# A row maximum over 64 MB: three blocks of rows per partition in place of two

## The chip, the core and the metric

The kernel runs on one core of a Trainium2 chip. The metric is the device time of one execution in microseconds (us), as the median of several runs. Lower is better.

## What is computed

The input `x` has the shape 32 x 512 x 1024 in float32 (67.11 MB). The output is the maximum over the last axis, 32 x 512 in float32.

```python
def reference(x):
    return np.max(x, axis=-1).astype(np.float32)
```

There are 16384 rows of 1024 values (4 KB each). Each value is read once, and one value per row is written.

## The kernel before, in words

**Layout.** The 16384 rows are dealt out to 128 partitions, so that each partition holds 128 rows. This is not done in one piece: the list `BLOCKS` (line 13) cuts the 128 rows of a partition into blocks. A block of S rows per partition covers 128 x S consecutive rows of `x`, and partition p gets rows p x S to p x S + S - 1 of it. So S decides the distance in `x` between the data of neighbouring partitions, the partition pitch: S x 4 KB. Before the change there are two blocks, of 112 rows (pitch 448 KB) and of 16 rows (14 in the list and 2 cut into pieces; pitch 64 KB).

**Loads.** Each number in a block's list is one load: so many rows of every partition, 128 runs of 4 KB times that number. Eighteen loads (line 238) and four pieces (line 243) are issued by SyncE's queue, in order. `loads[j]` is numbered from 0 through all blocks. The pieces are the last two rows, each cut in two by `PIECES` (line 26).

**The ring.** The loads go into `ring`, which has room for `RING = 47` rows per partition. Loads take places one behind another, and start again at 0 when the next one does not fit. `issue()` (line 231) sends the next load as soon as, in the written order of the program, all readers of the rows that it overwrites have been written down; on the chip SyncE then waits for those readers (VectorE's reductions) and for the earlier load into that place. A load that waits holds up all loads behind it in SyncE's queue.

**Work.** `PLAN` (line 31) is the written order of the steps: `d` reduces the rows of a load on VectorE (`direct`, a `reduce_max` on line 78), `t` moves some of the rows by TensorE, ScalarE and GpSimd instead (`turn`: transposes on line 160, a copy on line 166, an all-reduce over partitions on line 168), `b` brings these results back (line 178), `p` has VectorE reduce the remaining columns of a shared row, `m` merges, and `f0` to `f3` reduce the four pieces. `SHARED` and `RANK` say for loads 10, 13, 14 and 17 how many rows and how many of their eight column parts go the second way. The numbers in `PLAN`, `SHARED` and `RANK` are those of the loads in order, whatever block they are in.

**Stores.** Results of all rows stand in `res`, one column per row of a partition. `views` holds one store for each block. All but the last are issued on ScalarE's queue (line 265) and made to wait for the first piece's reduction (`behind`); the last (line 267) waits for the final merge.

The lines that cannot be said in words:

```python
BLOCKS = [
    [2, 15, 16, 14, 11, 11, 10, 10, 8, 8, 7],
    [3, 3, 3, 2, 1, 1, 1],
]
RING = 47
```

```python
for sizes in BLOCKS:
    S = sum(sizes) + last * (sizes is BLOCKS[-1])
    xb = xf[first * P:(first + S) * P, :].rearrange("(p i) d -> p i d", p=P)
    dst = bass.AP(tensor=of.tensor, offset=of.offset + first * P, ap=[[S, P], [1, S]])
    views.append((dst, res[:, first:first + S]))
```

Of the kernel before, what the change touches and what calls it, by code (L numbers as in the profile page):

```python
# [10 lines left out]


BLOCKS = [
    [2, 15, 16, 14, 11, 11, 10, 10, 8, 8, 7],
    [3, 3, 3, 2, 1, 1, 1],
]
RING = 47
# [279 lines left out]
```

## Time and profile before

| what | value |
|---|---|
| median of 3 runs | 163.83 us (163.79 to 163.84) |
| span of the profiled execution, first to last instruction | 162.1 us |
| DMA queue of the loads (q1) | 67.11 MB, 96.8% of the 16 engines' span |
| HBM read over the span | 67.11 MB; 414 GB/s with the stores |
| VectorE (DVE) busy | 135.3 us, 83% |
| GpSimd (POOL), TensorE (PE), ScalarE (ACT) busy | 15.9, 13.6 and 6.3 us |
| mean granted TensorE clock | 0.955 |

The profile is taken of one execution. Its span counts from the first instruction of the program to the last; the device time of an unprofiled run, 163.83 us, is 1.7 us longer, and what lies around the span is not in the trace. Engines are named PE (TensorE matmul), PEld (TensorE weight load), DVE (VectorE), ACT (ScalarE), POOL (GpSimd) and SP (SyncE); a q behind the name is the engine's instruction queue, where DMAs are issued. "L78" is line 78 of the kernel. A group's row has the line, the engine, the operation, output and input with their shapes, the count, then busy time and mean duration. A row of the timeline or the chain begins with its start and its duration in us. A row of DMA issues has the count, the KB of one, and the time in us from issue to landing. A row of windows has the stretch, its length, the busy time of PE, PEld, DVE, ACT and POOL, then the granted clock, the busy share of the DMA engines (above 1 where packets overlap or where their time reaches past the window) and GB/s.

### The profile page before, as it was taken

What the parts mean: (1) busy time and instruction counts of PE and PEld (TensorE: products, weight loads), DVE (VectorE), ACT (ScalarE), POOL (GpSimd) and SP (SyncE); (2) the same over time, 40 slices, a digit from 0 to 9 for tenths busy, and PEclk for the clock granted to TensorE, in tenths of its full rate; (3) what the DMA queues carried; (4) which work ended last, traced back from release to release, by engine and by line L of the source; (5) the groups of instructions that cost most, each with busy time, mean ns of one, the idle gap of its engine ahead of it and who ended that gap; (6) DMA issues with size and microseconds to landing.
All of it is one profiled execution on the core that took longest, in us unless ns stands there. A gap on an engine that the chain in (4) does not pass through costs nothing.

```text
span 162.1 us, 295 instructions
## 1 busy us (share of the span) xinstructions
PE 13.6 (8%) x76; PEld 11.7 (7%) x76; DVE 135.3 (83%) x33; ACT 6.3 (4%) x7; POOL 15.9 (10%) x10
## 2 busy tenths in 40 slices
PE   0000000000000000000000000000000000772942
PEld 0000000000000000000000000000000000762731
DVE  3500019998399999999999999996999999999994
ACT  3000000000000000000000000000000000241120
POOL 0000000000000000000000000000000000099791
PEclk9999999999999999999999999999999999996555
DMA  5995999599879999898999799799999989999991
GB/s 178 566 485 258 470 501 517 259 517 517 354 340 439 453 404 534 356 523 367 478 411 475 334 485 475 334 485 388 477 429 388 466 382 446 415 421 416 411 388 34
DMA packets 3456, 67.18 MB, mean 414 GB/s; under 512 B 640, under 2 KB 896, under 8 KB 1536
## 3 DMA queue, kind: packets, MB, share of 16 engines
q1 hardware_dynamic: 3168, 67.11, 96.8%
q10 hardware_dynamic: 288, 0.07, 0.2%
HBM read 67.11 MB, written 0.07 MB: 414 GB/s over the span
## 4 chain that ended last, share of the span: by engine, by line
DMA 50%; DVE 47%; SPq 1%; issue 0%; DVEq 0%
DMA ring<-in_x_dram 50%; DVE ring L78 45%; DVE joint L78 2%; SPq L238 1%; DVEq L292 0%
## 5 line engine op out<-in xcount | busy, mean ns | idle before, releaser
L78 DVE TENSOR_REDUCE ring<-ring 128x1 f32<-128x1024 f32 (+13 forms) x20 | 129.9, 6547 | 23.5 <-DMA ring<-in_x_dram 23.5
L168 POOL PARTITION_ALL_REDUCE top<-sb x6 | 15.7, 2658 | 142.6 <-ACT sb L166 142.5
L160 PE MATMUL ps<-ident,ring 128*128 128x128 f32 x38 | 9.0, 423 | 140.0 <-DMA ring<-in_x_dram 140.0
L160 PEld LDWEIGHTS ps<-ident,ring 128*128 128x128 f32 x38 | 7.6, 225 | 140.1 <-issue 140.1
L166 ACT COPY sb<-ps 128x1024 f32<-128x1024 f32 (+2 forms) x6 | 5.0, 834 | 150.5 <-PE ps L160 143.5
L78 DVE TENSOR_REDUCE joint<-ring 128x2 f32<-128x1280 f32 (+1 forms) x3 | 3.9, 1314 | 0.0
L178 PE MATMUL got<-ident,top 1*128 1x1 f32 x24 | 2.7, 228 | 3.8 <-POOL top L168 3.6
L178 PEld LDWEIGHTS got<-ident,top 1*128 1x128 f32 x24 | 2.4, 188 | 4.6 <-POOL top L168 4.6
L178 PE MATMUL joint<-ident,top 1*128 1x1 f32 x14 | 2.0, 244 | 1.9 <-POOL top L168 1.9
L178 PEld LDWEIGHTS joint<-ident,top 1*128 1x128 f32 x14 | 1.7, 210 | 2.7 <-POOL top L168 2.7
L166 ACT ACT_TABLE_LOAD x1 | 1.3, 1283 | 0.7 <-PEq L281 0.7
L83 DVE MEMSET ident<- 128x128 f32 x1 | 0.2, 165 | 0.8 <-PEq L281 0.8
L90 DVE TENSOR_SCALAR rowno<-rowno 32x1 f32<-32x1 f32 x3 | 0.4, 146 | 0.1
L85 DVE TENSOR_TENSOR_SCAN colno<-ident 128x128 f32<-128x128 f32 x1 | 0.4, 425 | 0.0
L92 DVE TENSOR_SCALAR ident<-colno,rowno 128x128 f32<-128x128 f32 x1 | 0.3, 288 | 0.0
L87 DVE STREAM_TRANSPOSE rowno<-colno 128x32 f32<-128x32 f32 x1 | 0.2, 211 | 0.0
L78 DVE TENSOR_REDUCE ring<-got 128x3 f32<-128x24 f32 x1 | 0.2, 172 | 0.0
L78 DVE TENSOR_REDUCE ring<-joint 128x5 f32<-128x20 f32 x1 | 0.2, 170 | 0.0
L281 POOL MEMSET const-float32-0.0<- 128x1 f32 x1 | 0.1, 98 | 0.2 <-issue 0.2
L281 POOL MEMSET const-bfloat16-1.0<- 128x1 bf16 x1 | 0.1, 102 | 0.0
L281 POOL MEMSET const-uint8-127<- 128x1 uint8 x1 | 0.1, 101 | 0.0
L281 POOL MEMSET const-float32-1.0<- 128x1 f32 x1 | 0.1, 98 | 0.0
(1 smaller groups left out, 0.1 us busy)
## 6 DMA issues: line engine op xcount, KB each, us to landing
ring<-in_x_dram SPq DMA_DIRECT2D x2, 5632.0 KB, 29.9
ring<-in_x_dram SPq DMA_DIRECT2D x2, 5120.0 KB, 36.8
ring<-in_x_dram SPq DMA_DIRECT2D x2, 4096.0 KB, 32.5
ring<-in_x_dram SPq DMA_DIRECT2D x1, 7680.0 KB, 22.6
ring<-in_x_dram SPq DMA_DIRECT2D x1, 7168.0 KB, 58.0
ring<-in_x_dram SPq DMA_DIRECT2D x3, 1536.0 KB, 35.7
ring<-in_x_dram SPq DMA_DIRECT2D x1, 3584.0 KB, 29.2
ring<-in_x_dram SPq DMA_DIRECT2D x2, 1024.0 KB, 17.8
```

The lines of the kernel that those rows point to most:

```text
L78: return in_turn("DVE", nc.vector.reduce_max(out=out, in_=in_, axis=X))
L83: in_turn("DVE", nc.vector.memset(ident, 1.0))
L85: in_turn("DVE", nc.vector.tensor_tensor_scan(out=colno, data0=ident, data1=ident, initial=-1.0, op0=ALU.add, op1=ALU.mult))
L87: in_turn("DVE", nc.vector.transpose(out=rowno, in_=colno[:, :32]))
L90: in_turn("DVE", nc.vector.tensor_scalar(out=part, in0=part, scalar1=float(q * 32), scalar2=None, op0=ALU.add))
L92: identity = in_turn("DVE", nc.vector.tensor_scalar(out=ident, in0=colno, scalar1=rowno[:, 0:1], scalar2=None, op0=ALU.is_equal))
L160: in_turn("PE", nc.tensor.transpose(out=ps[:, w:w + P], in_=rows(j)[:, lead[j] + r + i, c * P:(c + 1) * P], identity=ident,))
L166: in_turn("ACT", nc.scalar.copy(out=sb[:, :W], in_=ps[:, :W]))
L168: in_turn("POOL", nc.gpsimd.partition_all_reduce(top[:, :W], sb[:, :W], P, bass_isa.ReduceOp.max))
L178: in_turn("PE", nc.tensor.transpose(out=share(j)[:, r + i, c:c + 1], in_=tops[k][0:1, w:w + P], identity=ident[0:1, 0:1],))
L238: load = nc.sync.dma_start(out=rows(issued), in_=src)
L281: nc = _bacc.Bacc("TRN2", target_bir_lowering=False, num_devices=1)
```

## The change

The 112 rows of the first block are divided into a block of 16 rows and one of 96. The loads of the first block are now of 2 and 14 rows, and the second block begins with 16, 14 and 12 rows where 16, 14 and 11 stood. The numbers of the loads, `PLAN`, `SHARED`, `RANK`, the ring's size, the last block and the pieces stay as they are. Since each block has its own store, there are three stores in place of two. Every line below the list moves down by one (line 78 becomes 79, and so on).

```diff
 BLOCKS = [
-    [2, 15, 16, 14, 11, 11, 10, 10, 8, 8, 7],
+    [2, 14],
+    [16, 14, 12, 11, 10, 10, 8, 8, 7],
     [3, 3, 3, 2, 1, 1, 1],
 ]
 RING = 47
```

The partition pitch in `x` is 64 KB for loads 0 and 1, 384 KB for loads 2 to 10, and 64 KB for loads 11 to 17 and the pieces. The places in the ring move with the sizes: loads 0 to 3 take rows 0 to 46 of 47, load 4 (12 rows) begins again at 0, load 5 at 12, load 6 at 23, load 7 at 33, and load 8 at 0 again.

## The prediction

> **What bounds the kernel now.** I read the page first, for the share of the DMA queue and of the engines.
>
> ```profile
> span 162.1 us, 295 instructions
> PE 13.6 (8%) x76; PEld 11.7 (7%) x76; DVE 135.3 (83%) x33; ACT 6.3 (4%) x7; POOL 15.9 (10%) x10
> ...
> q1 hardware_dynamic: 3168, 67.11, 96.8%
> q10 hardware_dynamic: 288, 0.07, 0.2%
> ```
>
> The load queue (q1) keeps the sixteen DMA engines busy for 96.8% of the span; VectorE (DVE), the next, for 83%. So the stream of loads should be the bound, and VectorE only follows. The chain that ended last names VectorE for nearly half of its length, so I checked it in order of time.
>
> ```profile
> 1.62 41.49 DMA ring<-in_x_dram
> ...
> 43.13 66.55 DVE ring L78 x5
> ...
> 111.01 38.94 DMA ring<-in_x_dram
> ...
> 159.14 0.59 DVE ring L78
> 159.74 0.09 DVEq L292
> ```
>
> The 66.55 us on VectorE are a stretch in which both run; at its end VectorE's release lets SyncE issue four loads, and the last of them takes 38.94 us to land, behind others, so this link is not a lack of work in the queue. To see whether the queue ever runs dry I set the issue of each gated load (timeline of SyncE's queue) beside the landing of the load ahead of it (issue plus the time to landing, from the DMA view of the same stretch). Two answers of the DMA view, for the issues at 60.76 and at 75.37:
>
> ```profile
> ring<-in_x_dram SPq DMA_DIRECT2D x1, 5120.0 KB, 38.1
> ring<-in_x_dram SPq DMA_DIRECT2D x1, 5120.0 KB, 35.6
> ```
>
> They land at 98.9 and 111.0: 12.1 us apart for 10 rows, although they were issued 14.6 us apart. In the same way the load issued at 60.38 lands 26.3 us later, and its predecessor lands only at 39.96 + 33.4 = 73.4, 13 us after that issue. This is the smallest lead of all gated loads. The queue is never empty from the first packet to the last piece.
>
> What a row costs follows from the starts of the first reductions, each released by its load:
>
> ```profile
> 5.65 2.29 DVE L78 TENSOR_REDUCE ring<-ring 128x2 f32<-128x2048 f32 x1 [3.14 <-DMA ring<-in_x_dram]
> 23.78 16.15 DVE L78 TENSOR_REDUCE ring<-ring 128x15 f32<-128x15360 f32 x1 [15.85 <-DMA ring<-in_x_dram]
> 43.13 17.22 DVE L78 TENSOR_REDUCE ring<-ring 128x16 f32<-128x16384 f32 x1 [3.20 <-DMA ring<-in_x_dram]
> ```
>
> 15 rows take 23.78 - 5.65 = 18.13 us, 16 rows 19.35: the one extra row costs 1.22, and with the later sizes (12.1 for 10 rows) all fit about 1.2045 us a row plus 0.08 us a load. That is 0.524 MB per row at 435 GB/s.
>
> **The change, part by part.**
>
> *Sizes of the loads.* 15 and 11 rows become 14 and 12; every other size, and the number of loads (18 and four pieces), stays. By the rule above the second load lands at 5.62 + 14 x 1.2045 + 0.08 = 22.56 instead of 23.76, the third at 41.9, the fourth at 58.8, the fifth (12 rows) at 73.4. Before it was 73.4 too, because 15 + 16 + 14 + 11 = 14 + 16 + 14 + 12 = 56. From there on the stream is the same: 0 us.
>
> *VectorE.* Fifteen rows take 16.15, fourteen 15.08, eleven 11.88 us; twelve, between 11 and 14, 12.94. Sums: 28.03 before, 28.02 after. Nothing, and all of it beside loads.
>
> *When places in the ring come free.* The ring now places 2, 14, 16, 14 in rows 0 to 46, so load 6 (10 rows) overlaps the fourth load and must wait for its reduction, and load 7 goes right behind it. Reductions end at 22.57 + 15.08 = 37.7, 41.9 + 17.2 = 59.1, 74.2, 87.1, 98.9 and 109.7. Load 4 is issued at 37.7 (load 3 lands at 58.8), load 5 at 59.1 (load 4 at 73.4), load 6 at 74.2, which is 13.4 us later than before, but load 5 lands only at 86.7; loads 7 and 10 come earlier than needed. The smallest lead is 86.7 - 74.2 = 12.5 us, against 13 before. Cost 0, hidden behind load 5. If that cover were gone, the queue would pay the time from an issue to full flow, from 0.72 to about 3.2 us in the first load: up to 2.4 us once.
>
> *The third store.* ScalarE issues 16 columns, then 96, then the last 16. The two early ones go off behind the first piece's reduction, at 158.01; one issue is 0.38 us there, so both are out at 158.8, and the last store needs VectorE's final merge (159.66 + 0.17) and is issued at 159.86. One microsecond of cover on ScalarE's queue. On the engines q10 holds 0.2% of the span for two stores, 0.32 us, so 0.16 for one; if all of that went ahead of the last piece, it would cost 0.16, but the first store lands 1.6 us after its issue and the last piece at 159.0. SyncE's final check has one more semaphore to read. Taken: +0.02, bounds 0 and +0.16.
>
> *The partition pitch.* Three things change: the first two loads go from 448 KB to 64 KB, the following nine from 448 KB to 384 KB, the last seven stay at 64 KB. In full flow the trace holds both 448 and 64 KB: the first by the rows above, the second by the loads behind 138.9 us (3, 3, 3 and 2 rows, to 152.4): 13.5 us for 11 rows in four loads, while the rule gives 11 x 1.2045 + 4 x 0.08 = 13.6. A pitch of 64 KB is neither better nor worse there, to 0.1 us. So I take 384 KB, which lies between, at 0 as well.
>
> What the trace does not have is the *cold* start at 64 KB. The windows show how it goes at 448 KB (last two columns: DMA share, GB/s):
>
> ```profile
> 1.70:2.20 0.50, 0.00 (x0) 0.00 (x0) 0.44 (x3) 0.31 (x1) 0.00 (x0) 1.00 1.37 213
> 2.20:2.70 0.50, 0.00 (x0) 0.00 (x0) 0.29 (x1) 0.00 (x0) 0.00 (x0) 1.00 0.32 98
> 2.70:3.20 0.50, 0.00 (x0) 0.00 (x0) 0.00 (x0) 0.00 (x0) 0.00 (x0) 1.00 0.98 393
> 3.20:3.70 0.50, 0.00 (x0) 0.00 (x0) 0.00 (x0) 0.00 (x0) 0.00 (x0) 1.00 0.97 410
> 3.70:4.20 0.50, 0.00 (x0) 0.00 (x0) 0.00 (x0) 0.00 (x0) 0.00 (x0) 1.00 1.04 442
> 4.20:4.70 0.50, 0.00 (x0) 0.00 (x0) 0.00 (x0) 0.00 (x0) 0.00 (x0) 1.00 1.00 426
> ```
>
> Between 1.7 and 3.2 the engines begin (213 + 98 + 393) x 0.5 us = 352 KB, where 426 GB/s would be 639. The missing 287 KB are 0.67 us, lost once and never made up, because the stream is saturated from there to the end. This is all that the pitch can touch: if the pitch caused all of it, the gain is 0.67; if the new pitch makes it as bad again, the loss is 0.67. The nearest row is the switch from 448 to 64 KB at 138.9 us, at which the first touch of a new part of x costs nothing (the 0.1 us above); but there the queue was already flowing, so it speaks only weakly about the start. I take 0, and keep both ends.
>
> There is a rule against this part. The Trainium skill, "DMA: Bandwidth & Descriptors", section "Latency and other measured facts", says that HBM copies whose partition pitch is a large power of two lose rate: 207 GB/s at 512 KiB, 164 at 2 MiB, against 214 with a padded pitch. It names neither 64 nor 384 KB, and the trace has 64 KB at full rate; if the loss at 512 KiB (3.3%) fell on the 96 rows of the middle block, an estimate by that page would be 96 x 1.2 x 0.033 = 3.8 us slower.
>
> **Sum.** 0 + 0 + 0 + 0.02 + 0 on a span of 162.1 us. The median is 163.83, 1.7 us more than the span, which lies outside it and isn't touched; so 163.8.
>
> **The rivals.** *Faster start.* At 64 KB sixteen engines begin within a stretch of x seven times smaller, and the slow stretch from 1.7 to 3.2 shrinks. For it: the loss is there in the trace, and the changed loads are the ones in it. Against it: nothing shows that the pitch causes it rather than the first use of the queue. It needs half of the 0.67 to count, and gives 163.2 to 163.5.
>
> *Worse start, slower.* The same place, the other sign: 64 KB is itself a power of two, and if the engines' first reads collide more than at 448 KB (seven times 64), the first packets wait longer. Price up to +0.67, 163.8 to 164.5; it decides once the first load lands later than 5.62 + 0.33 = 5.95.
>
> *Middle block slower at 384 KB.* 96 rows are 96 x 1.2045 = 116 us of the bound, so each 1% of rate costs 1.16 us; from 0.3% on it decides. Against it: 448 and 64 KB agree to 0.1 us in 13.6. At 1%: 165.0.
>
> That the change does not do what it says I exclude: the first block has 16 rows per partition, and the order of the changed kernel's loads begins with 2 and 14 rows.
>
> **How the numbers follow.** I use 0.2% (0.33 us) as what a measurement of this kernel can tell from no change. No visible change: 0.53, with a range of its own of 163.5 to 164.15. Faster start beyond 0.33: 0.27. Worse start: 0.12. Middle block: 0.08. So faster 0.27, same 0.53, slower 0.20. The range for 8 in 10 takes in nearly all of the faster start, down to 163.2, and the lower half of the slower cases, up to 164.3; that leaves out some 0.04 below and 0.12 above.
>
> **What would show it.** The first reduction's start tells the cold start: 5.65 is no change, 5.3 the gain, over 5.95 the loss. The second should then start 16.93 us after it, the third 19.35 after that, and the load of 12 rows should land 14.5 us after its predecessor: longer gaps mean that the middle block reads slower. If the queue shows a hole between 74 and 99 us, my ring argument is wrong. The last piece should land where the start put it, and the last store 2.3 us later; if the start gains and the end does not, something behind 138.9 us has become the bound.

## The result, and the profile after

| kernel | median | lowest to highest | executions |
|---|---|---|---|
| before | 163.86 us | 163.73 to 164.04 | 21 |
| after | 164.13 us | 163.77 to 164.39 | 21 |

The ratio is 1.0013, with a 95% interval of 1.0007 to 1.0019: slower by some 0.2 us. This lies inside the 0.2% that the prediction called visible, but clear of no change, and I had forecast no change. The spread says more than the median. The executions of before lie within 0.31 us, those of after within 0.62, and the quickest are as quick as before. The profiled execution was the quickest of the 21 (163.77 us), so the first trace shows a changed kernel that is *faster*. Its page, with the rows that answer to those of before:

```profile
span 162.0 us, 295 instructions
...
q1 hardware_dynamic: 3168, 67.11, 96.9%
q10 hardware_dynamic: 432, 0.07, 0.2%
```

q10 carries 432 packets in place of 288, the third store; the load queue is as full as before. The timeline of VectorE for the first loads:

```profile
5.45 2.29 DVE L79 TENSOR_REDUCE ring<-ring 128x2 f32<-128x2048 f32 x1 [2.94 <-DMA ring<-in_x_dram]
22.39 15.09 DVE L79 TENSOR_REDUCE ring<-ring 128x14 f32<-128x14336 f32 x1 [14.66 <-DMA ring<-in_x_dram]
41.74 17.22 DVE L79 TENSOR_REDUCE ring<-ring 128x16 f32<-128x16384 f32 x1 [4.26 <-DMA ring<-in_x_dram]
```

The first reduction starts 0.20 us earlier than before (5.45 against 5.65), since its load lands at 5.43 instead of 5.62; the second starts 16.94 after it (forecast 16.93), the third 19.35 after that. The start is seen in the windows, where 246, 164 and 410 GB/s stand in place of 213, 98 and 393:

```profile
1.70:2.20 0.50, 0.00 (x0) 0.00 (x0) 0.44 (x3) 0.30 (x1) 0.00 (x0) 1.00 1.37 246
2.20:2.70 0.50, 0.00 (x0) 0.00 (x0) 0.28 (x1) 0.00 (x0) 0.00 (x0) 1.00 0.44 164
2.70:3.20 0.50, 0.00 (x0) 0.00 (x0) 0.00 (x0) 0.00 (x0) 0.00 (x0) 1.00 1.00 410
```

The chain that ended last is easier to read than before's:

```profile
1.62 40.10 DMA ring<-in_x_dram
...
41.74 32.22 DVE ring L79 x2
...
73.98 24.67 DMA ring<-in_x_dram
...
98.67 10.83 DVE ring L79
...
110.37 39.40 DMA ring<-in_x_dram
```

Load 2 lands at 41.72, two reductions later load 6 is issued and lands at 98.65, and load 13 lands at 110.37 + 39.40 = 149.77. Between loads 2 and 6 lie 47 rows in four loads: the rule of the prediction gives 47 x 1.2045 + 4 x 0.08 = 56.93, and the chain 98.65 - 41.72 = 56.93. Loads 7 to 13 take 51.12; before, from 98.82 to 149.95, they took 51.13. So this execution lost nothing in the middle block. All of its 0.1 us gain is the start, less a little at the end: from the landing of the last piece to the end of the span it is 3.13 us against 3.10 before. Where the slower executions, up to 0.6 us behind this one, lose their time, this trace does not say.

### The profile page after: what moved, and what is told of

Read it like the earlier page. It is cut to its first block, busy times and chain, and to the rows that moved or that the text cites. A ratio compares the mean times of both kernels' runs of the same rounds, so it can differ in the third digit from the quotient of the medians.

```text
span 162.0 us, 295 instructions
## 1 busy us (share of the span) xinstructions
PE 13.1 (8%) x76; PEld 11.3 (7%) x76; DVE 135.4 (84%) x33; ACT 6.3 (4%) x7; POOL 15.9 (10%) x10
## 4 chain that ended last, share of the span: by engine, by line
DMA 64%; DVE 32%; SPq 1%; issue 0%; DVEq 0%
DMA ring<-in_x_dram 64%; DVE ring L79 30%; DVE joint L79 2%; SPq L239 1%; DVEq L293 0%
```

## The experiments

Theory S: the cold start at 64 KB varies, and is what the longer executions lose. Theory B (later P): loads of the middle block at 384 KB are delayed. Theory C: the sizes, the later issue of load 6 or the third store.

Unless the text says otherwise, the variants are edits of the changed kernel. In those with a `READ`, the loads take their source from a hand-written access pattern. `READ` names a block and gives for it the first row read, the pitch of the reads in rows, the first row stored and the pitch of the store:

```diff
-        xb = xf[first * P:(first + S) * P, :].rearrange("(p i) d -> p i d", p=P)
+        at_row, pitch, to_row, to_pitch = READ.get(len(views), (first * P, S, first * P, S))
-        dst = bass.AP(tensor=of.tensor, offset=of.offset + first * P, ap=[[S, P], [1, S]])
+        xb = bass.AP(tensor=xf.tensor, offset=xf.offset + at_row * D, ap=[[pitch * D, P], [D, S], [1, D]])
+        dst = bass.AP(tensor=of.tensor, offset=of.offset + to_row, ap=[[to_pitch, P], [1, S]])
```

### Which part: pitch of the first block against pitch of the middle block

The changed kernel as it is:

> The changed kernel once more, for a second trace and to set the others beside it on one chip. The first comparison gave 164.13 us against 163.86 (ratio 1.0013), but its profiled execution had a span of only 162.0 us while the spans of its runs reach 162.6. Theory S (the start): the cold start at 64 KB varies from run to run, so a slower execution has its first reduction later than 5.65 us and everything behind it unchanged. Theory B (the middle block): the start is not later, and the 96 rows at a pitch of 384 KB take more than 1.2045 us a row, so the landing of the last load of that block comes more than 133.3 us after that of the first load. Both expect a ratio of 1.0007 to 1.002.

Sizes, ring and three stores of the changed kernel, read as one block of 112 rows:

```diff
+READ = {0: (0, 112, 0, 112), 1: (16, 112, 16, 112)}
```

> Sizes and three stores of the changed kernel, but both first blocks read at the pitch of 448 KB as before (row 112 p + i). It separates the pitch from the sizes, the ring and the third store. Theories S and B both expect the time of before: ratio 0.9997 to 1.0005, first reduction at 5.65. Theory C (the sizes, the later issue of load 6 or the third store cost it) expects the ratio of the changed kernel, 1.0013.

First block 64 KB, middle block 448 KB:

```diff
+READ = {1: (2048, 112, 2048, 96)}
```

> Changed kernel, with the first block at 64 KB and the middle block read at a pitch of 448 KB (from row 2048 on, so it reads other rows than it should, and the results of the middle block are those of other rows). Theory B expects that the loss goes: ratio at or below 1.0000, and 0.9988 if the early start of 5.45 us stays. Theory S expects it to stay slow, 1.0010 to 1.0018.

First block 448 KB, middle block 384 KB:

```diff
+READ = {0: (0, 112, 0, 16)}
```

> Changed kernel, with the first block read at a pitch of 448 KB (results of the first block are those of other rows) and the middle block at 384 KB. Theory B expects the loss of the changed kernel plus the slower start: ratio 1.0013 to 1.0030, first reduction at 5.65. Theory S expects the time of before, 0.9997 to 1.0005.

| first, middle pitch | median us | ratio to before (interval) | above 164.1 us | first landing |
|---|---|---|---|---|
| 64, 384 (changed kernel) | 163.95 | 1.0009 (1.0000 to 1.0017) | 3 of 12 | 5.54 |
| 448, 448 | 163.93 | 1.0004 (0.9995 to 1.0012) | 0 of 11 | 5.60 |
| 64, 448 | 163.88 | 1.0000 (0.9991 to 1.0009) | 0 of 11 | 5.43 |
| 448, 384 | 163.96 | 1.0010 (1.0002 to 1.0019) | 3 of 11 | 5.57 |

The medians lie close, so I count the executions above 164.1 us, which before has once in 149 over all comparisons. They follow the middle block's 384 KB (6 of 23 with it, none of 22 without), not the first block's 64. Theory S would have put them into the third row and not the fourth, theory C into the second; neither shows. The ratio of the fourth row, 1.0010, stays below the 1.0013 that theory B gave as its least.

The trace's records of single DMA packets (one packet is one partition's part of a load) show what goes wrong. Counting packets of 8 KB and more behind the start that take over 20 ns longer than the median of their size: before has none of them, and 448/448 has none. The changed kernel of this table has 50; a 44 KB packet of load 5, usually 1665 ns, took up to 1931, and packets of load 11, usually 460, up to 654. Half of the 50 lie in loads 11 and 12, the first two of the last block, which reads at 64 KB as it did before; so the delays reach past the middle block.

### Where an execution over 164.1 us loses its time

Three more executions of the changed kernel, unchanged, for their traces:

> The changed kernel again, for the trace of one more execution: 13 of its 33 executions took over 164.1 us, and none of those left a trace yet. Theory P: an execution over 164.1 has a first landing like the quick ones (5.4 to 5.6 us), packets over their usual time between 60 and 143 us, and the whole loss (0.2 to 0.6 us) between the landings of loads 3 and 11. Theory S: the loss is there at the first landing.

> As for the repetition before it: one more execution of the changed kernel. Theory P puts what an execution over 164.1 us loses between the landings of loads 3 and 11, theory S at the first landing.

> As for the repetitions before it: one more execution of the changed kernel. Theory P puts what an execution over 164.1 us loses between the landings of loads 3 and 11, theory S at the first landing.

All three were over it: 164.17, 164.29 and 164.26 us. (Of the 33 executions before them it was 14, not 13.) The chain of the second, the longest:

```profile
1.62 40.05 DMA ring<-in_x_dram
...
41.69 32.22 DVE ring L79 x2
...
73.93 24.92 DMA ring<-in_x_dram
...
98.88 10.83 DVE ring L79
...
110.58 39.70 DMA ring<-in_x_dram
```

Against the quick execution it is 0.05 us *ahead* at load 2 (41.67 against 41.72). Load 6 then needs 24.92 us to land instead of 24.67, and load 13 39.70 instead of 39.40. Its first reduction starts even earlier than that of the quick one:

```profile
5.42 2.29 DVE L79 TENSOR_REDUCE ring<-ring 128x2 f32<-128x2048 f32 x1 [2.92 <-DMA ring<-in_x_dram]
```

The other two chains read the same way, at load 6:

```profile
74.04 24.99 DMA ring<-in_x_dram
```

```profile
74.09 24.93 DMA ring<-in_x_dram
```

All six traces of the changed kernel, from the landings (the excess is over 56.93 and 51.12 us; the last row is of a later comparison, told below):

| execution, us | first landing | loads 3 to 6 | loads 7 to 13 |
|---|---|---|---|
| 163.77 | 5.43 | 0.00 | 0.00 |
| 163.93 | 5.54 | 0.00 | +0.04 |
| 164.17 | 5.51 | +0.33 | +0.01 |
| 164.29 | 5.40 | +0.26 | +0.31 |
| 164.26 | 5.57 | +0.26 | +0.12 |
| 164.17 | 5.64 | +0.19 | 0.00 |

So theory P holds and theory S falls: what an execution over 164.1 us loses, it loses in the middle block and at the switch to the last one. In the 164.29 case the two places are load 5 (13.58 us behind its predecessor instead of 13.32) and load 11 (4.03 instead of 3.69). In that load 5, 24 of the 128 packets were delayed, by up to 251 ns; the whole trace has 75 such packets, the quick one 22. The 75 delays add up to 6.9 us over all 16 engines. A load has landed when the last of its sixteen parts has: those of load 4 land within 0.34 us of each other, those of load 5 within 0.55, those of load 11 within 0.73, and of load 13 still within 0.68. So some engines fall behind the others and stay behind, and of the 6.9 us this execution loses 0.57; the three other traces over 164.1 us lose 0.19 to 0.38. In loads 2 to 10, the four traces over 164.1 us have 44 to 98 late packets, the two quicker ones 1 and 25. But the number alone does not tell the loss: the quickest execution has 21 more in loads 11 and 12, and loses nothing.

### Which pitches

388 KB (97 rows), to take the power of two out of 384:

```diff
+READ = {1: (2048, 97, 2048, 96)}
```

> Changed kernel with the middle block read at a pitch of 97 rows, 388 KB (from row 2048 on; its results are those of other rows). It leaves nearly the same distance between partitions as 384 KB and takes the factor of 128 KB out of it. Theory B1 (the collisions come from the power-of-two factor in the pitch, 128 KB in 384 KB): no run above 164.1, ratio 0.9990 to 1.0004, no packet of loads 2 to 10 longer than its kind. Theory B2 (any pitch other than the 448 KB of before brings them, or it is the distance itself): as the changed kernel, about one run in three above 164.1 and ratio 1.0009 to 1.0013.

512 KB (128 rows):

```diff
+READ = {1: (16, 128, 2048, 96)}
```

> Changed kernel with the middle block read at a pitch of 128 rows, 512 KB (from row 16 on; its results are those of other rows). Theory B1 expects the effect to grow with the power of two: ratio 1.002 to 1.03, delayed packets in every part of the middle block. Theory B2 expects what 384 KB did, 1.0009 to 1.0013.

388 KB took 163.92 us, ratio 1.0009 (1.0000 to 1.0018), 2 of 11 above 164.1, and its trace has 69 delayed packets, nearly all from 74 us on, though that execution (163.97 us) is not one of the slow ones. So theory B1, in which only the large power of two in the pitch collides, falls. 512 KB took 164.06 us, ratio 1.0017 (1.0007 to 1.0027), 4 of 8 above 164.1, a ratio between the forecasts of B2 and B1; its profiled execution (164.38) has 114 delayed packets, in loads 1 to 5 and none behind 75 us. Between loads 2 and 6 it loses 0.46 us; the chain at load 6:

```profile
74.14 25.12 DMA ring<-in_x_dram
```

It is no larger effect than 384 KB behind the same start. Then the sizes of before in blocks of 17, 95 and 16 rows (68, 380 and 64 KB), and of 2, 110 and 16 (8, 440 and 64 KB):

```diff
 BLOCKS = [
-    [2, 14],
-    [16, 14, 12, 11, 10, 10, 8, 8, 7],
+    [2, 15],
+    [16, 14, 11, 11, 10, 10, 8, 8, 7],
```

> Sizes of before, but divided into blocks of 17, 95 and 16 rows (2 and 15; 16, 14, 11 and so on), so the pitches are 68, 380 and 64 KB; the output is the full one. The early start of the changed kernel at 64 KB, 5.43 to 5.54 us against 5.62, is to be kept without a pitch of 384 KB. Theory B1: no slow runs; ratio 0.9988 to 1.0000 if a small pitch at the start is what makes it early, 1.0002 if it needs 64 KB exactly. Theory B2: ratio 1.0009 or more.

```diff
 BLOCKS = [
-    [2, 14],
-    [16, 14, 12, 11, 10, 10, 8, 8, 7],
+    [2],
+    [15, 16, 14, 11, 11, 10, 10, 8, 8, 7],
```

> Sizes of before, divided into blocks of 2, 110 and 16 rows, pitches 8, 440 and 64 KB; the output is the full one. The first load then reads one piece of 1 MB in order. If the closeness of the first reads makes the start early, the first reduction begins at or before 5.45 us, ratio 0.9985 to 1.0000. If the start needs distance between the engines, it begins after 5.65 and the ratio is over 1.0002. Theory B1 expects no slow runs, B2 some.

17, 95 and 16: 163.91 us, ratio 1.0006 (0.9997 to 1.0015), none above 164.1 and not one delayed packet, so not every pitch but 448 KB is bad, and B2 falls too (the ratio of 1.0009 that B2 forecast lies inside the interval, but the packets decide). Its start was late, at 5.71. 2, 110 and 16: 166.07 us, ratio 1.0134 (1.0120 to 1.0148), by something that I had not thought of. Its loads land as before's do; the loss is in the stores, as its DMA issues show:

```profile
out_dram<-ring ACTq DMA_DIRECT2D x1, 55.0 KB, 4.7
out_dram<-ring ACTq DMA_DIRECT2D x1, 1.0 KB, 3.0
out_dram<-ring ACTq DMA_DIRECT2D x1, 8.0 KB, 3.5
```

The first store has two columns, 8 bytes a partition, and takes 3.0 us to land; the two behind it take 4.7 and 3.5. In the changed kernel, where the narrowest store has 16 columns, they take 1.6 and 1.4:

```profile
out_dram<-ring ACTq DMA_DIRECT2D x1, 48.0 KB, 1.6
out_dram<-ring ACTq DMA_DIRECT2D x2, 8.0 KB, 1.4
```

Which store makes which slow is not shown by this run alone. Narrow runs that are no multiple of 64 bytes are not enough: in the kernel of 17, 95 and 16 rows, the stores with 68 and 380 bytes a partition take 1.6 and 1.8 us. That the store of 8 bytes holds up the two behind it is the likely reading.

Since the kernels of 17, 95 and 16 and of 2, 110 and 16 rows differ from the changed one in pitch, start and sizes, three more reads separate pitch and start, with the sizes of the changed kernel: 380 KB behind 64, 384 KB behind 68, and 440 KB behind 64.

```diff
+READ = {1: (2048, 95, 2048, 96)}      # 64, 380
+READ = {0: (0, 17, 0, 16)}            # 68, 384
+READ = {1: (2048, 110, 2048, 96)}     # 64, 440
```

> Changed kernel (first block at 64 KB) with the middle block read at a pitch of 95 rows, 380 KB, from row 2048 on; its results are those of other rows. The kernel with blocks of 17, 95 and 16 read at 380 KB too and had not one delayed packet, but began at 68 KB and with other sizes. Theory P1 (the pitch of the middle block alone decides): no delayed packets here either, no run above 164.1. Theory P2 (the start at 64 KB sets the engines' distances in time, and only together with them do some pitches collide): delayed packets as at 384 and 388 KB, and runs above 164.1.

> Changed kernel with the first block read at a pitch of 17 rows, 68 KB (its results are those of other rows) and the middle block at 384 KB. Theory P1: delayed packets in loads 2 to 11 and runs above 164.1, as with the start at 64 KB. Theory P2: hardly any, ratio 1.0000 to 1.0008.

> Changed kernel with the middle block read at a pitch of 110 rows, 440 KB, from row 2048 on; its results are those of other rows. A second pitch that was free of delays behind another start. Theory P1: free of delays, ratio 0.9995 to 1.0003. Theory P2: delays and runs above 164.1.

| first, middle pitch | median us | ratio (interval) | above 164.1 us | delayed packets in the trace |
|---|---|---|---|---|
| 64, 380 | 163.94 | 1.0006 (0.9997 to 1.0015) | 1 of 11 (164.13) | 1 |
| 68, 384 | 163.96 | 1.0010 (1.0001 to 1.0019) | 1 of 11 (164.37) | 1 |
| 64, 440 | 163.84 | 1.0001 (0.9992 to 1.0010) | 0 of 11 | 34 |

Neither P1 nor P2 comes out. 380 KB has one delayed packet behind a start at 64 KB, against P2, and 384 KB an execution of 164.37 behind 68 KB. 440 KB has 34 delayed packets here, 15 of them in the middle block, against P1; behind the start at 8 KB it had three, one of them in that block (of 23 ns). With 34 of them no execution was above 164.1, so late packets need not cost time. Over all executions, 384 KB behind a start at 64 KB was above 164.1 in 23 of 47, behind 448 or 68 KB in 4 of 22, and everything that read its middle part at 448 KB in 0 of 55 (apart from before itself). That the middle block's pitch matters is shown by these counts. That the start matters too is only suggested: on the one chip that ran 384 KB behind both 64 and 448 KB it was 3 of 12 against 3 of 11, and the counts of packets are of one trace each. Which pitches bring late packets behind which start, and why, stays open.

### The third store alone

The kernel before, with its first store cut in two:

```diff
-        views.append((dst, res[:, first:first + S]))
+        for u, v in [(0, 16), (16, S)] if sizes is not BLOCKS[-1] else [(0, S)]:
+            dst = bass.AP(tensor=of.tensor, offset=of.offset + first * P + u, ap=[[S, P], [1, v - u]])
+            views.append((dst, res[:, first + u:first + v]))
```

> The kernel before with nothing changed but its first store, cut into 16 and 96 columns: the third store alone. From the ends of the traces so far (3.13 to 3.15 us from the last landing to the end with three stores, 3.10 with two) it should cost 0.03 to 0.05 us, ratio 1.0002 to 1.0003. If the third store were the cause of the loss, ratio 1.0009 to 1.0016.

163.90 us against 163.84, ratio 1.0001 (0.9992 to 1.0010): not told from nothing, and not the cause.

### A form without the bad pitch

The first block as in the changed kernel, and all the rest as one block of 112 rows at 448 KB, its store cut at column 96 (the lines that cut it are left out here):

```diff
 BLOCKS = [
     [2, 14],
-    [16, 14, 12, 11, 10, 10, 8, 8, 7],
-    [3, 3, 3, 2, 1, 1, 1],
+    [16, 14, 12, 11, 10, 10, 8, 8, 7, 3, 3, 3, 2, 1, 1, 1],
```

> The first block as in the changed kernel (2 and 14 rows, 64 KB), and everything behind it as one block of 112 rows at a pitch of 448 KB, whose store is cut at column 96 so that there are three stores as in the changed kernel; the output is the full one. The run with the middle block at 448 KB (median 163.88, none above 163.99) says that this pitch keeps the packets free of delays behind a start at 64 KB except at the switch into the last block, and here there is no such switch. Theory P (packets delayed by the pitch behind the start are what makes the changed kernel slower): first reduction at 5.40 to 5.60, no run above 164.1, ratio 0.9985 to 1.0000. Theory S (the start at 64 KB varies and costs it): runs above 164.1 as with the changed kernel, ratio 1.0005 to 1.0015.

> The blocks of 16 and 112 rows with the store cut at column 96 once more, beside the changed kernel on one chip. On the first chip it took 163.79 us against 163.87 of before, with none of 11 runs above 164.01, but its interval (0.9989 to 1.0007) does not tell it from before. If its start at 64 KB gains some 0.1 us and nothing is lost behind it, ratio 0.9992 to 1.0000 and no run above 164.1; if the first chip was luck, runs above 164.1 as in the changed kernel.

> The changed kernel on the same chip: 17 of its 36 executions so far were above 164.1, between 3 of 12 on one chip and 3 of 3 on another. Theory P1 (the pitch of 384 KB): 3 to 8 of about 11 above 164.1, ratio 1.0005 to 1.0020, and a profiled execution that loses its time in loads 3 to 11 again.

The form took 163.79 us (ratio 0.9998, 0.9989 to 1.0007) and, on another chip, 163.91 (1.0000, 0.9991 to 1.0009), none of 22 executions above 164.1. The changed kernel beside it on that second chip took 164.14 (1.0016, 1.0007 to 1.0025), 6 of 11 above. The two chains at load 6, first this form, then the changed kernel:

```profile
73.98 24.66 DMA ring<-in_x_dram
```

```profile
74.20 24.84 DMA ring<-in_x_dram
```

With the first block left at 64 KB and the 384 KB gone, the loss is gone. The form is as good as before, not better by anything that could be measured.

## Why the prediction was right or wrong

**The step that failed** is "So I take 384 KB, which lies between, at 0 as well". I argued from two pitches of the trace to a third between them, as if the price were a smooth function of distance. It is not. Behind a start at 64 KB, the traces with 448 KB have no more than six late packets in the loads at that pitch, and those with 380 KB none; in loads 2 to 10, those with 384 KB have from 1 to 98, with 388 KB 29 and with 512 KB 113. Packets of the loads at 64 KB right behind a block of 384 KB are late as well, so that the full rate of 64 KB in the trace of before did not carry over either. I had the place among the rivals (middle block, 0.08) but with the wrong mechanism, a steady loss of rate on all 96 rows. What the traces show are separate delays of some packets, which cost nothing in one execution and 0.2 to 0.6 us in another, and some 0.2 us in the median. One profiled execution of a kernel whose trace has none of them could not price them, and 0 to 1.16 us should have been carried as this term's bounds.

**The rule of the Trainium skill** ("DMA: Bandwidth & Descriptors", "Latency and other measured facts"), that large powers of two in the partition pitch cost rate in copies between HBM tensors, pointed at the right part but not at the size. By its loss at 512 KiB I had put an estimate of 3.8 us; reading the 96 rows at 512 KB gave a ratio of 1.0017, some 0.2 to 0.3 us. And the delays do not need a large power of two in the pitch, since 388 KB (97 x 4 KB) has them.

**The start.** I took 0, with 0.67 at either end. First landings at 64 KB lie between 5.40 and 5.64 in the six traces of the changed kernel (mean 5.51), at 448 KB between 5.48 and 5.62 in four (mean 5.57): a mean gain of 0.05 us (0.07 over all thirteen traces that begin at 64 KB, mean 5.50), which so few traces do not tell from nothing. By the windows, the time lost before 3.2 us (0.67 before) is 0.54 to 0.62 in these six and 0.65 to 0.69 in the four at 448 KB: the slow stretch shrinks by some 0.1 us in the mean, of which about half shows at the first landing. The rival of a worse start is out; that of a faster start has the right sign, but in the mean a tenth of its price of 0.67. Against the one trace of before, single traces of the changed kernel lie from 0.22 us earlier to 0.02 later.

**Sizes, ring, VectorE: right.** Load 4 is issued at 37.5 and load 6 at 74.0, and the queue has no hole; with both blocks ahead of the last at 448 KB no packet is late. The load of 12 rows lands 14.54 us behind its predecessor, forecast 14.5.

**The third store: right to the order.** From the last piece's landing to the end of the span it is 3.13 to 3.16 us in the traces of the changed kernel, against 3.10 before: 0.03 to 0.06, forecast 0.02; ScalarE's cover held:

```profile
157.83 0.86 ACTq L266 DMA_DIRECT2D out_dram<-ring  x2
```

```profile
159.69 0.34 ACTq L268 DMA_DIRECT2D out_dram<-ring  x1
```

The two early stores are issued by 158.69, one microsecond ahead of the last.

**The sum, corrected** for the longest traced execution: start -0.22, loads 3 to 6 +0.26, loads 7 to 13 +0.31, end +0.04, together +0.39; its span is 162.5 against 162.1.

## What to carry to other kernels

When a stream of loads is the bound and full, a change of its addresses can be a change of the bound: price a pitch that the trace does not have with bounds, not with the mean of its neighbours. When the executions of a kernel spread more widely than those of the one before, take several traces before explaining: the one at hand may be the quickest, and show the opposite sign. And when cutting an output into blocks, look at the width of the narrowest store.

## What the runs showed of the hardware

- With all sixteen DMA engines busy, single packets were late by up to 0.28 us depending on the partition pitch in HBM (384, 388, 440 and 512 KB behind a start at 64 KB), and so were packets of the next two loads at 64 KB behind a block of 384, 388 or 440 KB, and up to 9 packets behind one of 448 KB. Those at 448 KB kept their usual time to 20 ns in the trace of before, in the variants 448/448 and 64/448 and with the cut store, and only 5 or 6 were late in the two traces of the form with 16 and 112 rows. Why they are late is not shown.
- A store of 8 bytes for each of 128 partitions took 3.0 us to land, and the store of 440 bytes behind it 4.7; stores of 64 and 68 bytes took 1.4 and 1.6, of 380 and 384 bytes 1.8 and 1.6. Whether the width or the neighbouring addresses do it was not tried.
- The cold start of the load queue lost 0.5 to 0.8 us in every trace, reckoned as in the prediction: 0.52 to 0.64 with the first load at 64 KB, 0.67 at 8 KB, 0.65 to 0.69 at 448 KB, 0.69 and 0.81 at 68 KB.
